# Score products over four column groups, a later first score episode, and pinned head work in a hybrid decoder layer

## The chip, the cores and the metric

The kernel runs on one NeuronCore of a Trainium2 chip. The metric is the device time of one execution in microseconds (us), lower is better. Engines are named as in the profile: PE is TensorE (matmuls, and PEld its weight loads), DVE is VectorE, ACT is ScalarE, POOL is GpSimd, SP is SyncE, which here only issues transfers.

## The reference, cut to what matters

One decoder layer on 1024 tokens of width 1024, all in 32-bit floats:

```python
x = x + hybrid_mixer(rms_norm(x, norm_mix), ...)                 # this half holds the change
x = x + square(relu(rms_norm(x, norm_mlp) @ w_up)) @ w_down
return rms_norm(x, norm_final)

# in hybrid_mixer
proj = h @ w_in                       # split into xa, ga, q, f, v, g, m_a, m_b, 1024 wide each
y_a = rg_lru(conv(xa), ...) * gelu(ga)
qf, kf = silu(q), (1 - lb) * sigmoid(-f);  log_f = log(lb + (1 - lb) * sigmoid(f))
o = rms_norm(hgrn2_chunkwise(qf, kf, log_f, v), hg_norm)         # 8 heads of 128
y = sigmoid(m_a) * y_a + sigmoid(m_b) * (o * silu(g))
return y @ w_out

# hgrn2_chunkwise, for each chunk of a head
o_inter = (q * exp(cum)) @ state
scores  = sum_k q[t] * k[s] * exp(cum[t] - cum[s])   for s <= t
o       = o_inter + scores @ v
state   = exp(last) * state + (k * exp(last - cum)).T @ v
```

The kernel uses chunks of 128 tokens instead of 32.

## The kernel before, in words

The tokens are done in two halves of 512 (`c` = 0, 1). In each half, four pairs of heads (`p` = 0 to 3) are done one after the other: these are the eight **stages**. A stage projects, in this order, `xa`, `q`, `f` (with the gates of the recurrent unit inside), `g`, `mb`, `ga` and `ma`; `v` is projected before every second stage. A projection (`project`) is 48 matmuls of 128x128 weights on 128x512 inputs: weights and inputs are split into a high and a low part, and each product is three matmuls (`mm3`, lines 121 to 123). It is two weight tiles ("halves") of eight **column groups**, where a group is one `mm3`, so three matmuls. The weights come by DMA, are cast on ACT (line 82, `wH`) and their low part is taken on DVE (line 83, `wL`).

The chunked recurrence is the generator `hgrn`. `gates` runs it in pieces between column groups: `next(scores)` once at its start, and then `project(c, name, at, do)` calls `go_on` after the group with number `at`. Its pieces before the change:

- Start: products of queries, keys and decays on DVE (line 467, a helper), up to the last part of `qa`.
- After group 8 of `mb`, the **first score episode**: 2 x 32 small matmuls (line 475; keys of 32 columns against 48 query columns), each writing a strip of 32 of a bank's 128 rows, chosen by `32 * b`. Then the two levels of `dd` masks on DVE (lines 490 to 499), the next level's `qb`, `kb`, `kk` (the keys, also called `kw`), `qn` (its last part is `q3`, line 572), `ke`.
- After group 7 of `ga`, everything else: the **second score episode** (lines 577 to 585: `p64` with 16 products 64 columns wide on strips 0 and 1, then `p8` with 32 products 48 wide on all four strips, then `p32` with 16 products 32 wide on strips 0 and 2), the third level's `dd` masks, copies into the score tile `scT` (POOL for `dd`, ACT for `p32` and `p64`), two DVE products and an ACT copy into `kk` (lines 603 to 605), `qf`; then for each head in turn the key transposes `pk` (line 623, copied to `kT` by ACT), key-value products `pkv` (line 629), outputs `po` (lines 636 and 639) and state updates `sn`, `scar` (lines 643 and 645).

What sets the order: a planner at build time orders each engine's instructions by priority and by its own estimate of when inputs are ready. `high_priority(300)` puts a piece run by `go_on` ahead of what was written up to 300 places before it. `turn` (`tc.keep_in_program_order`) pins an instruction behind the one written just before it on its engine; instructions written later may still be moved ahead of it. Score products are pinned; `pk`, `pkv`, `po` and the projections are not. On the chip each engine works through its order and waits where an input is late. PSUM banks (2 KB a partition): four with the tag `pj` for projections, two `sc`, two `hg`, each handed on when its last reader is done. `kT`, `sn`, `kb` are tiles with one buffer each.

Of the kernel before, what the change touches and what calls it, by code (L numbers as in the profile page):

```python
# [14 lines left out]
ALU = mybir.AluOpType  # L15
# [3 lines left out]
P = 128  # L19
D = 1024  # L20
S = 1024
T = 512
# [20 lines left out]
def trunk(ctx: ExitStack, tc: tile.TileContext, x, wts, mlp, pv, gains, mask_f, mask_u, out):  # L43
# [142 lines left out]
    def small_inputs():  # L186
        nc.sync.dma_start(pvt, pv[:, 0:PV_N])
        nc.sync.dma_start(mf, mask_f)
        mu32 = mt("kT", "mu32", (P, 4, P)).rearrange("p a b -> p (a b)")[:, : 7 * 32]
# [155 lines left out]

    def project(c, name, at=None, do=None):

        pp = [bank("pj", f"pj_{name}_{s}") for s in range(2)]
        for half in range(2):
            wh, wl = next_w()  # L350
            for k in range(4):
                hh, hl = kt(hT[c], 4 * half + k)
                for s in range(2):
                    cols = slice(k * 256 + s * P, k * 256 + (s + 1) * P)
                    mm3(pp[s], wh[:, cols], wl[:, cols], hh, hl, half == 0 and k == 0, half == 1 and k == 3)
                    if at == 8 * half + 2 * k + s:
                        do()
        return pp
# [105 lines left out]
    def hgrn(c, p, q1, f, kk, v):  # L464
# [131 lines left out]

        for b in (0, 2):
            A.copy(scT[32 * b : 32 * b + 32, :, 32 * b + 32 : 32 * b + 64], p32[32 * b : 32 * b + 32, :, :])
        A.copy(scT[0:64, :, 64:128], p64[0:64, :, :])
        t16 = t64.rearrange("p (a e) -> p a e", e=2)  # L600
        before = t16[:, :, 0:1].unsqueeze(3).to_broadcast([P, 8, 2, 32])
        after = t16[:, :, 1:2].to_broadcast([P, 8, 32])
# [14 lines left out]
        nkv = 3 if c + 1 == NC else 4  # L617
        pos = []
        for s in range(2):
            u = 2 * p + s  # L620
            pk = bank("hg", f"pk{c}{u}")
            for n in range(nkv):
                PE.transpose(pk[:, n * P : (n + 1) * P], kk[:, s * T + n * P : s * T + (n + 1) * P], ident)
            kT = mt("kT", f"kT{c}{u}", (P, 4, P))
            A.copy(kT[:, :nkv, :], pk[:, : nkv * P].rearrange("p (n k) -> p n k", n=nkv))
            pkv = bank("hg", f"pkv{c}{u}")
            vn = lambda n: v[:, n, (u % 4) * P : (u % 4 + 1) * P]
            for n in range(nkv):
                PE.matmul(pkv[:, n * P : (n + 1) * P], kT[:, n, :], vn(n), start=True, stop=True)
            sn = mt("sn", f"sn{c}{u}", (P, 3, P))  # L630
            state = lambda n: scar[:, u, :] if n in (0, 4) else sn[:, n - 1, :]
            po = bank("hg", f"po{c}{u}")
            for n in range(4):
                only = c == 0 and n == 0
                on_ps = po[:, n * P : (n + 1) * P]
                PE.matmul(on_ps, scT[:, 4 * s + n, :], vn(n), start=True, stop=only)
                if not only:
                    at = s * T + n * P
                    PE.matmul(on_ps, qf[:, at : at + P], state(n), start=False, stop=True)  # L639
                if n < nkv:  # L640
                    kv = pkv[:, n * P : (n + 1) * P]
                    if only:
                        V.tensor_copy(state(1), kv)
                    else:
                        V.scalar_tensor_tensor(
                            state(n + 1), state(n), t128[:, 4 * s + n : 4 * s + n + 1], kv, op0=ALU.mult, op1=ALU.add
                        )
            for n in range(4):
# [10 lines left out]
    def gates(c, p, h, scores, dst):  # L659
# [505 lines left out]
```

## Time and profile before

| | |
|---|---|
| median of 3 runs | 1599.73 us (1597.9 to 1602.51) |
| profiled execution | 1600.96 us, of which its span 1599.2 |
| PE busy | 1564.1 us, 98% of the span, 9002 matmul records |
| DVE busy | 1200.7 us, 75% |
| ACT busy | 784.9 us, 49% |
| DMA | 245.97 MB, mean 154 GB/s |
| mean granted TensorE clock | 0.996 |

A busy share is of one engine over the whole span. A row of a timeline gives start, duration, engine, line, operation, output and inputs with shapes, how many such instructions in a row were merged, and in brackets the idle time of the engine before it and what ended it. A row of the waits gives who waited for whom, the total, how often, and the longest. A matmul of 32-bit floats that are not split has two records; a split one has one.

### The profile page before, as it was taken

What the parts mean: (1) busy time and instruction counts of PE and PEld (TensorE: products, weight loads), DVE (VectorE), ACT (ScalarE), POOL (GpSimd) and SP (SyncE); (2) the same over time, 40 slices, a digit from 0 to 9 for tenths busy, and PEclk for the clock granted to TensorE, in tenths of its full rate; (3) what the DMA queues carried; (4) which work ended last, traced back from release to release, by engine and by line L of the source; (5) the groups of instructions that cost most, each with busy time, mean ns of one, the idle gap of its engine ahead of it and who ended that gap; (6) DMA issues with size and microseconds to landing.
All of it is one profiled execution on the core that took longest, in us unless ns stands there. A gap on an engine that the chain in (4) does not pass through costs nothing.

```text
span 1599.2 us, 22797 instructions
## 1 busy us (share of the span) xinstructions
PE 1564.1 (98%) x9002; PEld 1284.6 (80%) x9002; DVE 1200.7 (75%) x1748; ACT 784.9 (49%) x1241; POOL 74.7 (5%) x105
## 2 busy tenths in 40 slices
PE   9999999999999999999999997999999999999998
PEld 7788888787788888788788876888888878888886
DVE  5876954958652867846869687988788888888875
ACT  5644544546432644445445566766777731221115
POOL 1010000010000010000000000000000000000002
PEclk9999999999999999999999998999999999999999
DMA  6222222222243222222222362666666666666652
GB/s 233 88 80 92 93 68 92 97 76 93 80 167 136 93 67 92 93 80 92 80 80 93 127 206 102 252 254 254 240 244 256 227 261 233 256 247 249 254 222 106
DMA packets 57995, 245.97 MB, mean 154 GB/s; under 512 B 6816, under 2 KB 6944, under 8 KB 47136
## 3 DMA queue, kind: packets, MB, share of 16 engines
q1 hardware_dynamic: 56304, 239.27, 41.0%
q10 hardware_dynamic: 1584, 5.25, 0.9%
q8 instruction: 70, 1.15, 0.3%
q14 instruction: 37, 0.30, 0.1%
HBM read 184.72 MB, written 59.77 MB: 153 GB/s over the span
## 4 chain that ended last, share of the span: by engine, by line
PE 84%; DVE 12%; ACT 1%; issue 1%; DMA 1%; POOL 0%; SPq 0%; DVEq 0%; ACTq 0%; POOLq 0%
PE dX L121 3%; PE dX L123 3%; PE dX L122 3%; PE uX L121 3%; PE uX L122 3%; PE uX L123 3%; DVE wL L83 2%; PE pj_xa L122 2%; PE pj_ma L123 2%; PE pj_xa L121 2%; PE pj_ma L121 2%; PE pj_ma L122 2%; PE pj_xa L123 2%; PE pj_f L121 2%; PE pj_f L123 2%; PE pj_f L122 2%
## 5 line engine op out<-in xcount | busy, mean ns | idle before, releaser
L83 DVE TENSOR_TENSOR wL<-raw,wH 128x1024 fp32r<-128x1024 f32 x158 | 193.5, 1225 | 134.2 <-ACT wH L82 133.8
L82 ACT CAST wH<-raw 128x1024 fp32r<-128x1024 f32 x160 | 167.8, 1049 | 177.9 <-issue 38.8
L1075 DVE TENSOR_TENSOR acc<-acc,dX 128x512 f32<-128x512 f32 x128 | 86.8, 685 | 29.3 <-PE dX L123 29.3
L82 ACT CAST wA<-q 128x512 fp32r<-128x512 f32 x32 | 19.8, 621 | 128.7 <-PE dX L123 81.4
L1075 DVE TENSOR_TENSOR acc<-acc,dY 128x512 f32<-128x512 f32 x64 | 43.4, 685 | 16.0 <-PE dY L123 13.9
L428 DVE RECIPROCAL rr<-rr 128x512 f32<-128x512 f32 x16 | 53.6, 3347 | 0.0
L932 ACT ACTIVATE b<-b 128x512 f32<-128x512 f32 x48 | 30.2, 630 | 37.2 <-DVE b L931 37.2
L1036 POOL TENSOR_TENSOR acc<-acc,gain 128x512 f32<-128x512 f32 x8 | 10.4, 1298 | 610.9 <-ACT junk L1033 610.6
L649 ACT ACTIVATE on<-po 128x128 f32<-128x128 f32 x64 | 16.8, 277 | 44.2 <-PE po L639 44.2
L394 DVE SCALAR_TENSOR_TENSOR xc<-xp,pvt,xc 128x512 f32<-128x512 f32 x48 | 33.1, 747 | 0.0
L539 POOL TENSOR_SCALAR seg<-seg 128x128 f32<-128x128 f32 (+1 forms) x16 | 16.7, 1045 | 340.2 <-DVE seg L467 340.2
L933 ACT ACTIVATE b<-b 128x512 f32<-128x512 f32 x48 | 30.1, 630 | 1.1
L123 PE MATMUL pj_mb<-hT0H,wL 128*128 128x512 f32 x64 | 25.0, 391 | 1.5 <-issue 1.5
L122 PE MATMUL pj_ga<-hT0H,wH 128*128 128x512 f32 x64 | 25.8, 402 | 0.4 <-issue 0.4
L123 PE MATMUL pj_ga<-hT1H,wL 128*128 128x512 f32 x64 | 26.1, 407 | 0.0
L121 PE MATMUL uX<-h2B11L,wA 128*128 128x512 f32 x64 | 25.5, 399 | 0.3 <-DVE rstd_h L147 0.3
L121 PE MATMUL pj_ga<-hT0L,wH 128*128 128x512 f32 x64 | 25.8, 403 | 0.0
L123 PE MATMUL pj_ga<-hT0H,wL 128*128 128x512 f32 x64 | 25.7, 402 | 0.0
L121 PE MATMUL pj_ga<-hT1L,wH 128*128 128x512 f32 x64 | 25.4, 397 | 0.0
L121 PE MATMUL po<-wL,y0H 128*128 128x512 f32 x64 | 25.3, 398 | 0.1
L121 PE MATMUL pj_mb<-hT0L,wH 128*128 128x512 f32 x64 | 25.4, 397 | 0.0
L121 PE MATMUL pj_mb<-hT1L,wH 128*128 128x512 f32 x64 | 25.4, 396 | 0.0
(1889 smaller groups left out, 5203.4 us busy)
## 6 DMA issues: line engine op xcount, KB each, us to landing
raw<-wts_in SPq DMA_DIRECT2D x160, 512.0 KB, 3.3
q<-mlp_in SPq DMA_DIRECT2D x64, 512.0 KB, 3.6
x<-x_in SPq DMA_DIRECT2D x8, 512.0 KB, 5.8
acc<-x ACTq DMA_DIRECT2D x8, 512.0 KB, 5.9
y_out<-acc SPq DMA_DIRECT2D x16, 256.0 KB, 2.1
xs<-x_in SPq DMA_DIRECT2D x8, 256.0 KB, 4.2
x<-xs SPq DMA_DIRECT2D x8, 256.0 KB, 2.0
x2s<-x_in SPq DMA_DIRECT2D x4, 512.0 KB, 5.4
```

The costliest lines, as they stand in the source:

```text
L82: keep(A.copy(h, src))
L83: keep(engine.tensor_tensor(out=lo, in0=src, in1=h.bitcast(F32), op=ALU.subtract))
L121: keep(PE.matmul(o, ah, bl, start=first, stop=False, **how))
L122: keep(PE.matmul(o, ah, bh, start=False, stop=False, **how))
L123: keep(PE.matmul(o, al, bh, start=False, stop=last, **how))
L394: V.scalar_tensor_tensor(xc[:, s, :], xp[:, j : j + T], pvt[:, PV_CW + 8 * j + u : PV_CW + 8 * j + u + 1], xc[:, s, :], op0=ALU.mult, op1= ...
L428: V.reciprocal(rec, rec)
L539: G.tensor_scalar(after[:, :, 2], t4[:, :, 3], 1.0, 0.0, op0=ALU.mult, op1=ALU.add)
L649: A.activation(on[:, 4 * s + n, :], po[:, n * P : (n + 1) * P], AF.Square, accum_out=ssq[:, 4 * s + n : 4 * s + n + 1])
L932: A.activation(b[:, at, :], b[:, at, :], AF.Relu, scale=-1.0 if at == 2 else 1.0)
L933: A.activation(b[:, at, :], b[:, at, :], AF.Square)
L1075: V.tensor_tensor(out=dst, in0=dst, in1=banks[bk, pr], op=op)
```

## The change

- `project` takes a tuple of group numbers. The first score episode runs after group 10 of `mb` instead of 8. The second one stays after group 7 of `ga`, and the generator has three more stops: the transposes of both heads after group 9, the key-value products of both after 11, the outputs of both after 13.
- The second episode is one loop over eight blocks; in each, two 32-wide, two 64-wide and four 48-wide products, and `p64` now uses strips 1 and 3. The copy of `p64` into `scT` becomes two copies of 32 rows.
- The DVE products and the ACT copy into `kk` and the copies of `p32` are written ahead of the third level's masks.
- `pk`, `pkv` and `po` matmuls are pinned in written order. `pkv` uses `sc` banks; `kT` of both heads is one tile in the place of `kb`; `sn` holds both heads' states, and six state updates come ahead of the outputs (the last of each head behind them).
- The small mask `mu32` lands in the tile `sn` instead of `kT`.

```diff
-    def project(c, name, at=None, do=None):
+    def project(c, name, at=(), do=None):
...
-                    if at == 8 * half + 2 * k + s:
+                    if 8 * half + 2 * k + s in at:
                         do()
...
         p64 = bank("sc", f"sc64_{nm}").rearrange("p (n t) -> p n t", n=8)
+        p32 = bank("hg", f"sc32_{nm}")[:, :256].rearrange("p (n t) -> p n t", n=8)
+        p8 = bank("sc", f"sc8_{nm}")[:, : 8 * 48].rearrange("p (n t) -> p n t", n=8)
         for n in range(8):
-            for j, keys in ((0, ke[:, 2 * n, :]), (1, kw[:, 4 * n + 1, :])):
-                small(p64[32 * j : 32 * j + 32, n, :], keys, q3[:, n, 1:3, :])
-        p8 = blocks(kb, rhs, str(cw))
-        p32 = bank("hg", f"sc32_{nm}")[:, :256].rearrange("p (n t) -> p n t", n=8)
-        for n in range(8):
-            for b in (0, 2):
-                small(p32[32 * b : 32 * b + 32, n, :], kw[:, 4 * n + b, :], qv[:, 4 * n + b + 1, :])
+            k = 4 * n
+            small(p32[0:32, n, :], kw[:, k, :], qv[:, k + 1, :])
+            small(p64[32:64, n, :], ke[:, 2 * n, :], q3[:, n, 1:3, :])
+            small(p32[64:96, n, :], kw[:, k + 2, :], qv[:, k + 3, :])
+            small(p64[96:128, n, :], kw[:, k + 1, :], q3[:, n, 1:3, :])
+            for b in range(4):
+                small(p8[32 * b : 32 * b + 32, n, :], kb[:, 32 * (k + b) : 32 * (k + b) + 32], rhs(k + b))
...
+        mul(kw[:, 1::4, :], kw[:, 1::4, :], after)
+        mul(kw[:, 0::4, :], ke[:, 0::2, :], after)
+        A.copy(kw[:, 2::4, :], ke[:, 1::2, :])
+        for b in (0, 2):
+            A.copy(scT[32 * b : 32 * b + 32, :, 32 * b + 32 : 32 * b + 64], p32[32 * b : 32 * b + 32, :, :])
         level(li, cw, p8)
...
-        A.copy(scT[0:64, :, 64:128], p64[0:64, :, :])
...
-        mul(kw[:, 0::4, :], ke[:, 0::2, :], after)
-        mul(kw[:, 1::4, :], kw[:, 1::4, :], after)
-        A.copy(kw[:, 2::4, :], ke[:, 1::2, :])
+        for j in range(2):
+            A.copy(scT[32 * j : 32 * j + 32, :, 64:128], p64[64 * j + 32 : 64 * j + 64, :, :])
...
-            kT = mt("kT", f"kT{c}{u}", (P, 4, P))
-            pkv = bank("hg", f"pkv{c}{u}")
-            sn = mt("sn", f"sn{c}{u}", (P, 3, P))
...
+        sn = mt("sn", f"sn{nm}", (P, 6, P))
+        kT = mt("kb", f"kT{nm}", (P, 8, P))
...
+        yield
+        for s, u in enumerate(us):
+            pk = bank("hg", f"pk{c}{u}")
+            for n in range(nkv):
+                turn(PE.transpose(pk[:, n * P : (n + 1) * P], kk[:, s * T + n * P : s * T + (n + 1) * P], ident))
+            A.copy(kT[:, 4 * s : 4 * s + nkv, :], pk[:, : nkv * P].rearrange("p (n k) -> p n k", n=nkv))
+        yield
+        for s, u in enumerate(us):
+            pkvs.append(bank("sc", f"pkv{c}{u}"))
+            for n in range(nkv):
+                small(pkvs[s][:, n * P : (n + 1) * P], kT[:, 4 * s + n, :], vn(u, n))
+        for s in range(2):
+            for n in range(3):
+                step(s, n)
+        yield
+        for s, u in enumerate(us):
+            po = bank("hg", f"po{c}{u}")
...
+                turn(PE.matmul(on_ps, scT[:, 4 * s + n, :], vn(u, n), start=True, stop=only))
...
+                    turn(PE.matmul(on_ps, qf[:, at : at + P], state(s, n), start=False, stop=True))
+            if nkv == 4:
+                step(s, 3)
...
-        pb = project(c, f"mb{c}{p}", 8, go_on)
+        pb = project(c, f"mb{c}{p}", (10,), go_on)
...
-        pa = project(c, f"ga{c}{p}", 7, go_on)
+        pa = project(c, f"ga{c}{p}", (7, 9, 11, 13), go_on)
```

More of the change, by code (lines that the diff above doesn't have):

```diff
@@ L188, in small_inputs @@
         nc.sync.dma_start(mf, mask_f)
[L189 removed]
+        mu32 = mt("sn", "mu32", (P, 6, P)).rearrange("p a b -> p (a b)")[:, : 7 * 32]
         mu32 = mu32.rearrange("p (i b t) -> p i b t", i=7, b=1)
@@ L595, in hgrn @@
             )
[L597 to L602, printed above, removed]
-        mul(kw[:, 0::4, :], ke[:, 0::2, :], after)
-        mul(kw[:, 1::4, :], kw[:, 1::4, :], after)
-        A.copy(kw[:, 2::4, :], ke[:, 1::2, :])
+        for j in range(2):
+            A.copy(scT[32 * j : 32 * j + 32, :, 64:128], p64[64 * j + 32 : 64 * j + 64, :, :])
         qf = mt("q1", f"qf{nm}", (P, 1792))[:, 0:1024]
@@ L617, in hgrn, with step @@
         nkv = 3 if c + 1 == NC else 4
-        pos = []
-        for s in range(2):
-            u = 2 * p + s
+        us = (2 * p, 2 * p + 1)
+        vn = lambda u, n: v[:, n, (u % 4) * P : (u % 4 + 1) * P]
+        sn = mt("sn", f"sn{nm}", (P, 6, P))
+        state = lambda s, n: scar[:, us[s], :] if n in (0, 4) else sn[:, 3 * s + n - 1, :]
+        kT = mt("kb", f"kT{nm}", (P, 8, P))
+        pkvs = []
+        def step(s, n):
+            kv = pkvs[s][:, n * P : (n + 1) * P]
+            at = 4 * s + n
+            if c == 0 and n == 0:
+                V.tensor_copy(state(s, 1), kv)
+            else:
+                V.scalar_tensor_tensor(
+                    state(s, n + 1), state(s, n), t128[:, at : at + 1], kv, op0=ALU.mult, op1=ALU.add
+                )
+        yield
+        for s, u in enumerate(us):
             pk = bank("hg", f"pk{c}{u}")
             for n in range(nkv):
-                PE.transpose(pk[:, n * P : (n + 1) * P], kk[:, s * T + n * P : s * T + (n + 1) * P], ident)
-            kT = mt("kT", f"kT{c}{u}", (P, 4, P))
-            A.copy(kT[:, :nkv, :], pk[:, : nkv * P].rearrange("p (n k) -> p n k", n=nkv))
-            pkv = bank("hg", f"pkv{c}{u}")
-            vn = lambda n: v[:, n, (u % 4) * P : (u % 4 + 1) * P]
-            for n in range(nkv):
-                PE.matmul(pkv[:, n * P : (n + 1) * P], kT[:, n, :], vn(n), start=True, stop=True)
-            sn = mt("sn", f"sn{c}{u}", (P, 3, P))
-            state = lambda n: scar[:, u, :] if n in (0, 4) else sn[:, n - 1, :]
+                turn(PE.transpose(pk[:, n * P : (n + 1) * P], kk[:, s * T + n * P : s * T + (n + 1) * P], ident))
[3 more added lines that the diff above has]
+            pkvs.append(bank("sc", f"pkv{c}{u}"))
+            for n in range(nkv):
+                small(pkvs[s][:, n * P : (n + 1) * P], kT[:, 4 * s + n, :], vn(u, n))
[4 more added lines that the diff above has]
+        for s, u in enumerate(us):
             po = bank("hg", f"po{c}{u}")
```

13 lines of the change are left out of this document (3 added, 10 removed).

## The prediction

> **What bounds the kernel now.** I read the page first, then the waits of TensorE (PE), then the timelines of PE, VectorE (DVE) and ScalarE (ACT) in one of the eight stages (one per half of the sequence and pair of heads).
>
> ```profile
> span 1599.2 us, 22797 instructions
> PE 1564.1 (98%) x9002; PEld 1284.6 (80%) x9002; DVE 1200.7 (75%) x1748; ACT 784.9 (49%) x1241; POOL 74.7 (5%) x105
> PE sc L475 <- DVE qa L467: 6.5, 7, 0.9
> PE pk L623 <- DVE dd L499: 3.1, 7, 0.5
> ```
>
> PE is busy for 98% of the span, so PE time taken out shortens the kernel as long as no other engine's work becomes late. The two waits are at the first score episode and at the key transposes. A matmul's listed duration runs past the start of the next, so listed idle understates a wait; I take starts. PE in the third stage (start, duration):
>
> ```profile
> 302.05 0.39 PE L123 MATMUL pj_mb<-hT0H,wL 128*128 128x512 f32 x1
> ...
> 302.73 0.39 PE L123 MATMUL pj_mb<-hT0H,wL 128*128 128x512 f32 x1
> 304.07 0.88 PE L475 MATMUL sc<-qa,kb 128*32 128x48 f32 x63 [0.95 <-DVE qa L467]
> 304.75 0.21 PE L475 MATMUL sc<-q,kk 128*32 128x48 f32 x1
> 305.57 0.51 PE L121 MATMUL pj_mb<-hT0L,wH 128*128 128x512 f32 x1
> ...
> 315.69 0.39 PE L123 MATMUL pj_ga<-hT0H,wL 128*128 128x512 f32 x1
> 316.00 0.24 PE L475 MATMUL sc<-qn,ke 128*32 128x64 f32 x1
> ...
> 316.82 0.24 PE L475 MATMUL sc<-qb,kb 128*32 128x48 f32 x2
> 316.87 0.22 PE L475 MATMUL sc<-qn,ke 128*32 128x64 f32 x1
> ...
> 317.58 0.69 PE L475 MATMUL sc<-qn,kk 128*32 128x32 f32 x32
> 318.20 0.50 PE L121 MATMUL pj_ga<-hT0L,wH 128*128 128x512 f32 x1
> 318.53 0.39 PE L122 MATMUL pj_ga<-hT0H,wH 128*128 128x512 f32 x1
> ...
> 319.23 0.40 PE L122 MATMUL pj_ga<-hT0H,wH 128*128 128x512 f32 x1
> 320.07 0.63 PE L623 MATMUL pk<-ident,kk 128*128 128x128 f32 x4 [0.45 <-DVE dd L499]
> 320.46 0.48 PE L123 MATMUL pj_ga<-hT0H,wL 128*128 128x512 f32 x1
> ...
> 321.24 0.40 PE L123 MATMUL pj_ga<-hT0H,wL 128*128 128x512 f32 x1
> 321.48 1.06 PE L629 MATMUL pkv<-v,kT 128*128 128x128 f32 x8
> ```
>
> A projection matmul starts every 0.227 us (three steps from 302.05 to 302.73); a column group is three of them, 0.68. Where no input is late, a score episode starts 0.31 after the last projection matmul (315.69 to 316.00). After small work the second projection matmul comes 0.33 after the first (318.20 to 318.53), not 0.227: each return costs 0.1.
>
> DVE and ACT in the same stage:
>
> ```profile
> 303.22 0.70 DVE L467 TENSOR_TENSOR qa<-qa,seg 128x512 f32<-128x512 f32 x1
> ...
> 313.49 0.69 DVE L467 TENSOR_TENSOR qn<-qn,seg 128x512 f32<-128x512 f32 x1
> ...
> 316.96 1.23 DVE L83 TENSOR_TENSOR wL<-raw,wH 128x1024 fp32r<-128x1024 f32 x1 [1.48 <-ACT wH L82]
> 318.11 0.42 DVE L467 TENSOR_TENSOR kk<-kk,seg 128x256 f32<-128x256 f32 x1
> 318.44 0.37 DVE L499 COPY_PREDICATED dd<-mu,sc 128x192 f32<-128x192 uint8 x1
> ...
> 319.51 0.42 DVE L467 TENSOR_TENSOR kk<-ke,seg 128x256 f32<-128x256 f32 x1
> ...
> 317.14 0.58 ACT L599 COPY scT<-sc 64x512 f32<-64x512 f32 x1 [0.21 <-PE sc L475]
> 317.85 0.41 ACT L608 COPY qf<-qn 128x256 f32<-128x256 f32 x1
> 318.16 0.40 ACT L609 COPY qf<-qn 128x256 f32<-128x256 f32 x1
> 318.47 0.73 ACT L598 COPY scT<-sc 32x256 f32<-32x256 f32 x2
> ```
>
> **The change, part by part.**
>
> (a) First episode two groups (six matmuls) later. Today it should start at 302.73 + 0.31 = 303.04, but waits for the product into qa, which ends at 303.92, and starts 0.15 later at 304.07: 1.03 lost. Six matmuls later it would arrive at 303.04 + 6 x 0.227 = 304.40, 0.33 after its inputs. Here are the first and the last of the eight:
>
> ```profile
> 92.50 0.39 PE L123 MATMUL pj_mb<-hT0H,wL 128*128 128x512 f32 x1
> 93.12 0.29 PE L475 MATMUL sc<-qa,kb 128*32 128x48 f32 x7 [0.23 <-ACT wH L82]
> ...
> 869.84 0.39 PE L123 MATMUL pj_mb<-hT1H,wL 128*128 128x512 f32 x1
> 871.15 0.25 PE L475 MATMUL sc<-qa,kb 128*32 128x48 f32 x5 [0.93 <-DVE qa L467]
> ```
>
> The first stage loses 0.62 - 0.31 = 0.31, the last 1.00; with the seven alike, 0.31 + 7 x 1.03 = 7.5 us. What is late next would be the second episode, since there are now 39 matmuls between the two, not 45. It needs q3, the last part of qn, ready on DVE at 313.49 + 0.69 + 0.15 = 314.33. It would arrive at 304.40 + 1.50 (episode, 304.07 to 305.57) + 0.10 (return) + 39 x 0.227 + 0.08 = 314.93: 0.6 in hand. The DVE work that waits for the first episode (kb rewritten, then the first dd) follows a whole weight split; the episode ends 0.33 later than today, so I cost that at nothing, DVE's backlog being its cover; without that cover it costs up to 0.33 a stage.
>
> (b) Second episode over four column groups. Its keys are 32 columns wide, and the strip of 32 output rows they write is their column group. Today 16 products 64 wide run on two strips (316.00 to 316.82: 0.102 each per strip, eight on each), 32 products 48 wide on four (first half of the first episode, 304.07 to 304.75: 0.085), 16 products 32 wide on two (317.58 to 318.20: 0.077). In all 2.20. Dealt to four strips, the busiest holds eight of 64 and eight of 48: 8 x (0.102 + 0.085) = 1.50. That strips run by themselves, with mixed widths and two PSUM banks, shows at 316.82: 48-wide products start before the last 64-wide ones (316.87), on the strips these leave free. Bounds: an even load over the strips, 8 x (0.102 + 0.085 + 0.077 + 0.085)/2 = 1.40; all one after the other, 16 x 0.102 + 32 x 0.085 + 16 x 0.077 = 5.6. I take 1.50, nearest to the overlap seen: 8 x 0.70 = 5.6 us. One row pair speaks for a floor per record instead: the 64-wide part starts 32 records in 0.82, 26 ns each; against it, the first episode starts 128 in 1.50 us, 12 ns each. The Trainium skill (TensorE: Matmul & The Clock Gate, "Wait — 56ns, not 53.3ns?") has such a floor: matmul starts never fall below some 25 ns, however small the matmul. By that page, as an estimate, 128 records take 3.2 us and the sum would end 13.6 us higher; by the first episode it stays as it is, so the trace does not agree with the floor where four strips are in use.
>
> (c) Key transposes. Without a wait they would start at 319.23 + 0.24 (the entry at 321.24 to 321.48) = 319.47; they start at 320.07, since DVE, after a weight split that ends at 318.19, puts dd and qf work between its two kk products, the second of which ends at 319.93. So 0.60 a stage is lost. After: DVE's two kk products are issued ahead of dd and qf. The split hangs on ACT's cast, and that on PE's half of ga, so it still ends 2.19 after the episode's start; the first kk product starts at 2.11 (318.11 less 316.00), the second 0.33 on, as dd does now, and ends 0.42 later at 2.86, seen at 3.01. PE, with an episode of 1.50 and now six matmuls in between, arrives at 1.50 + 0.33 + 4 x 0.227 + 0.24 = 2.98. Nearly even; 8 x 0.60 = 4.8 us. What goes behind the kk products, dd and qf, comes up to 0.7 later; what waits for it is under (e).
>
> (d) Pinning. Both heads' transposes, then both key-value products, then both outputs, each after its own two groups. The same matmuls, but in the first half of the sequence four runs of projections instead of six after the second episode, 2 x 0.1 x 4 stages = 0.8 us. In the second half there are four now: nothing.
>
> (e) New waits. Eight transposes take 2 x 0.39 (320.07 to 320.46), and with a return and six matmuls the key-value products arrive at 2.98 + 0.78 + 0.10 + 1.36 = 5.2. They need kT. The score copy of 64 rows becomes two of 32, each at most the 0.58 of the old; ACT then has kk, two small scT copies, two large and two qf copies, 0.31 (the step from one qf copy to the next) + 0.73 + 1.16 + 0.62 = 2.8, from 1.65 after the episode's start to 4.5, and a first kT copy of the same width as the old 0.58 ends at 5.1. Nearly even. Then:
>
> ```profile
> 322.90 0.73 DVE L645 SCALAR_TENSOR_TENSOR sn<-sn,seg,pkv 128x128 f32<-128x128 f32 x2
> 320.22 1.78 POOL L588 TENSOR_SCALAR scT<-dd 32x256 f32<-32x256 f32 x4 [15.82 <-DVE dd L499]
> ```
>
> Four key-value products take 1.06 (321.48), so the second head's end at 5.2 + 2.12 = 7.3; three state updates of 0.37 behind them end at 8.4. The first output arrives at 7.3 + 0.1 + 1.36 = 8.8, and only the second head's outputs need the last updates. POOL's copies of dd end at 6.0 today and at most 0.7 later, 2 us ahead. So the new waits are between nothing and one order turned round, 0.6 a stage, as today's at pk. I take the low end, since all of these come out in hand, and allow 0.1: 0.8 us. No DMA is issued or moved, one small mask load merely lands in another tile; SP's queue and POOL's order stay.
>
> Sum: 7.5 + 5.6 + 4.8 + 0.8 - 0.8 = 17.9 us. The profiled execution took 1600.96 us, with 1.8 around its span of 1599.2; that gives 1583.1. It lies 1.2 above the median of 1599.73, so for the median 1582.
>
> **Rivals.**
>
> DVE keeps its order. The planner puts dd and qf between the two kk products as today. They then end 3.9 after the episode's start, PE arrives at 2.98: with the 0.15 to be seen, a wait of 1.05 a stage. That takes 8.4 back: 1590. For it: that is today's order. Against: both are traced ahead of dd now, and become ready with it.
>
> The wait moves to the second episode. A second weight split (1.23) falls into DVE's chain ahead of q3: 1.23 - 0.6 = 0.6 a stage, 4.9 in all, 1587; two splits 1.9 a stage, 1597. For it: DVE idles nowhere from the recurrent gates to q3. Against: splits are timed by PE, which moves the same way.
>
> The other side: strips of unlike width or bank do not overlap, each product waits for the one before. Then the episode takes 5.6, 3.4 more than today instead of 0.7 less: 1582 + 8 x 4.1 = 1615. It decides from 2.20 + 12.3/8 = 3.7 us on. Against it stand 316.82 and 316.87.
>
> A floor per record. If the dealt order keeps the 26 ns a record of today's 64-wide part, it takes 128 x 0.026 = 3.3: 1582 + 8 x 1.8 = 1596. Against it: the first episode's 12 ns.
>
> The pins do not give the written order. Projections written behind a pinned product may still be moved ahead of it. If the pieces drift so that (a), (c) and (d) bring nothing, (b) is left: 1599.7 - 5.6 = 1594; with (e) at its bound of 0.6 a stage, 1599. For it: today the transposes stand after the fifth matmul, not at a group's end. Against: both pinned episodes stand exactly where they are written.
>
> **How the numbers follow.** Forecast 0.70, its own range 1577 to 1587 (the runs shown spread 1597.9 to 1602.5, and (e) may cost nothing or twice what I allow). DVE order 0.12. Second episode late 0.06. Serial strips 0.05. Floor 0.02. Pins 0.05. The range 1576 to 1592 holds the first two and a part of the third. 0.3% of this kernel is 4.8 us, about what a measurement tells from no change: faster 0.70 + 0.12 + 0.05 (a late second episode short of 1595) = 0.87; same 0.06, from the floor and most of the pins; slower 0.07, the serial strips and the rest.
>
> **What would show it.** In the timeline after: the first episode 0.31 after its last matmul, in all eight stages; the second in about 1.5 us, 32-, 64- and 48-wide products mixed; transposes after six matmuls with no idle before; eight transposes, then two groups, and so on; the wait of sc for qa gone from the list and pk's near nothing. The prediction is wrong if sc waits for qn, if pk or pkv wait for kk or kT by over 0.5 us a stage, or if the second episode takes over 2 us.

## The result, and the profile after

The median fell from 1600.07 us (four runs, the three given above among them, 1597.9 to 1602.51) to 1584.14 us (four runs, 1582.06 to 1584.83), a ratio of 0.9891 with a 95% interval of 0.9879 to 0.9904. The forecast was 1582, its range 1576 to 1592. The profiled execution of the changed kernel took 1582.06 us with a span of 1579.3, 19.9 less than the span before.

The page of the changed kernel, and from PE's waits the rows at the places in question; the waits of `sc` for `qa` and of `pk` for `dd` are not in the list any more:

```profile
span 1579.3 us, 22822 instructions
PE 1554.5 (98%) x9002; PEld 1281.2 (81%) x9002; DVE 1199.7 (76%) x1748; ACT 789.4 (50%) x1249; POOL 75.0 (5%) x105
PE sc L475 <- DVE qn L467: 1.5, 2, 1.0
```

The kernel does the same work in the same number of matmul records, and PE is listed as busy for 98% of the span in both: a matmul's listed duration hides part of a wait, so what went shows in the starts. So I add up each stage from the start of its first `mb` matmul to the start of its first `ma` matmul. The third stage, PE, before:

```profile
296.84 0.39 PE L121 MATMUL pj_mb<-hT0L,wH 128*128 128x512 f32 x1
...
330.45 0.39 PE L121 MATMUL pj_ma<-hT0L,wH 128*128 128x512 f32 x1
```

and after:

```profile
292.60 0.39 PE L121 MATMUL pj_mb<-hT0L,wH 128*128 128x512 f32 x1
...
299.85 0.39 PE L123 MATMUL pj_mb<-hT0H,wL 128*128 128x512 f32 x1
300.17 0.89 PE L475 MATMUL sc<-qa,kb 128*32 128x48 f32 x64
...
310.41 0.39 PE L123 MATMUL pj_ga<-hT0H,wL 128*128 128x512 f32 x1
310.73 0.22 PE L475 MATMUL sc<-qn,kk 128*32 128x32 f32 x1
...
311.80 0.22 PE L475 MATMUL sc<-qn,ke 128*32 128x64 f32 x1
...
312.00 0.22 PE L475 MATMUL sc<-qn,ke 128*32 128x64 f32 x1
...
312.44 0.50 PE L121 MATMUL pj_ga<-hT0L,wH 128*128 128x512 f32 x1
...
313.71 0.40 PE L123 MATMUL pj_ga<-hT0H,wL 128*128 128x512 f32 x1
313.94 1.04 PE L642 MATMUL pk<-ident,kk 128*128 128x128 f32 x8
...
315.97 0.39 PE L123 MATMUL pj_ga<-hT0H,wL 128*128 128x512 f32 x1
316.19 1.95 PE L475 MATMUL pkv<-v,kT 128*128 128x128 f32 x16
...
319.13 0.39 PE L123 MATMUL pj_ga<-hT0H,wL 128*128 128x512 f32 x1
319.36 0.60 PE L658 MATMUL po<-v,scT 128*128 128x128 f32 x4
...
323.85 0.39 PE L121 MATMUL pj_ma<-hT0L,wH 128*128 128x512 f32 x1
```

The stage took 33.61 us before (330.45 - 296.84) and takes 31.25 now. The first episode starts 0.32 after the last matmul before it (299.85 to 300.17), so nothing is late. The second takes 1.71 (310.73 to 312.44); its 64-wide products on one strip repeat every 0.197 (311.80 to 312.00). Transposes, key-value products and outputs each start 0.22 or 0.23 after the matmul before them, which is the step between two projection matmuls: no wait at any of the three.

DVE in the same stage:

```profile
311.70 1.23 DVE L83 TENSOR_TENSOR wL<-raw,wH 128x1024 fp32r<-128x1024 f32 x1 [0.35 <-ACT wH L82]
312.84 0.42 DVE L467 TENSOR_TENSOR kk<-ke,seg 128x256 f32<-128x256 f32 x1
313.18 0.42 DVE L467 TENSOR_TENSOR kk<-kk,seg 128x256 f32<-128x256 f32 x1
313.51 0.37 DVE L499 COPY_PREDICATED dd<-mu,sc 128x192 f32<-128x192 uint8 x1
313.77 0.69 DVE L467 TENSOR_TENSOR qf<-qn,seg 128x512 f32<-128x512 f32 x1
```

The two `kk` products start 2.11 and 2.45 after the episode's start (310.73) and stand ahead of `dd` and `qf`, as the change writes them.

Summed over the stages, before: 32.89, 33.59, 33.61, 35.36, 33.73, 33.81, 33.77, 33.81, together 270.57 us. After: 31.25, 31.25, 31.25, 33.08 and four times 31.08, together 251.15. That is 19.4 of the 19.9 us that the span lost; nothing outside the stages moved by much. The medians differ by 15.9. The profiled execution is the shortest of the four; the other three had spans of 1581.2 to 1583.1 and left no trace, so where their 2 to 4 us lie is open.

The fourth stage stands out, 1.8 longer than its neighbours. PE there, then DVE:

```profile
402.67 0.39 PE L123 MATMUL pj_ga<-hT0H,wL 128*128 128x512 f32 x1
403.58 0.22 PE L475 MATMUL sc<-qn,kk 128*32 128x32 f32 x2 [0.53 <-DVE qn L467]
404.79 0.22 PE L475 MATMUL sc<-qn,ke 128*32 128x64 f32 x1 [0.98 <-DVE qn L467]
```

```profile
394.84 1.29 DVE L149 SCALAR_TENSOR_TENSOR xn<-x,rstd_x,gain 128x1024 f32<-128x1024 f32 x1 [0.53 <-POOL rstd_x L148]
...
403.36 0.68 DVE L467 TENSOR_TENSOR ke<-kk,seg 128x512 f32<-128x512 f32 x1
403.96 0.68 DVE L467 TENSOR_TENSOR qn<-qn,seg 128x512 f32<-128x512 f32 x1
```

The first norm of the second half (line 149, 1.29 us, behind 0.53 of idle until POOL has taken the norm's power, line 148) fell into DVE's chain between the two episodes. `q3`, the last `qn`, ends at 404.64, about 1.8 later than PE wanted it, and the episode starts late and then stops.

### The profile page after: what moved, and what is told of

Its sections match the earlier page's. It is cut to its first block, busy times and chain, and to the rows that moved or that the text cites. A ratio compares the mean times of both kernels' runs of the same rounds, so it can differ in the third digit from the quotient of the medians.

```text
span 1579.3 us, 22822 instructions
## 1 busy us (share of the span) xinstructions
PE 1554.5 (98%) x9002; PEld 1281.2 (81%) x9002; DVE 1199.7 (76%) x1748; ACT 789.4 (50%) x1249; POOL 75.0 (5%) x105
## 4 chain that ended last, share of the span: by engine, by line
PE 91%; DVE 6%; DMA 2%; issue 1%; ACT 1%; POOL 0%; SPq 0%; DVEq 0%; POOLq 0%
PE dX L121 4%; PE dX L123 3%; PE dX L122 3%; PE uX L121 3%; PE uX L123 3%; PE uX L122 3%; PE pj_ga L121 2%; PE pj_ma L123 2%; PE pj_xa L121 2%; PE pj_ma L122 2%; PE pj_ma L121 2%; PE pj_xa L122 2%; PE pj_xa L123 2%; PE pj_f L121 2%; PE pj_f L123 2%; PE pj_f L122 2%
## 5 line engine op out<-in xcount | busy, mean ns | idle before, releaser
L122 PE MATMUL uX<-h2B11H,wA 128*128 128x512 f32 x64 | 25.5, 398 | 0.0
L123 PE MATMUL uX<-h2B11H,wA 128*128 128x512 f32 x64 | 25.4, 396 | 0.0
L121 PE MATMUL po<-wL,y1H 128*128 128x512 f32 x64 | 25.2, 394 | 0.0
L121 PE MATMUL pv<-wL,hT1H 128*128 128x512 f32 x64 | 25.1, 394 | 0.0
```

The lines of the kernel that those rows point to most:

```text
L121: keep(PE.matmul(o, ah, bl, start=first, stop=False, **how))
L122: keep(PE.matmul(o, ah, bh, start=False, stop=False, **how))
L123: keep(PE.matmul(o, al, bh, start=False, stop=last, **how))
```

## The experiments

Ratios are against the kernel before on the same chip; the rows come from several chips, so compare ratios and not medians. Stage sums come from starts as above, in the one traced execution of each kernel. "First half" is a plain stage there (the third, or the first where that is disturbed), "second half" the seventh.

| kernel | ratio (95%) | median us | first half | second half | eight stages |
|---|---|---|---|---|---|
| before | 1 | 1600.07 | 33.61 | 33.77 | 270.57 |
| after | 0.9891 (0.9879 to 0.9904) | 1584.14 | 31.25 | 31.08 | 251.15 |
| late_only | 0.9955 (0.9942 to 0.9969) | 1594.6 | 32.58 | 32.79 | 263.33 |
| dealt_only | 0.9960 (0.9947 to 0.9974) | 1595.43 | 32.76 | 32.88 | 264.50 |
| at8 | 0.9925 (0.9909 to 0.9941) | 1588.48 | 32.30 | 32.10 | 257.07 |
| two_strips | 0.9932 (0.9918 to 0.9947) | 1589.57 | 31.95 | 31.76 | 257.06 |
| masks_first | 0.9914 (0.9897 to 0.9930) | 1586.95 | 31.57 | 31.35 | 254.43 |
| no_pins | 0.9922 (0.9907 to 0.9936) | 1587.51 | 32.14 | 31.91 | 258.45 |
| at12 | 0.9917 (0.9897 to 0.9938) | 1587.54 | 31.62 | 31.45 | 256.36 |
| norm_pinned | 0.9902 (0.9885 to 0.9919) | 1585.68 | 31.25 | 31.03 | 251.09 |
| strips_even | 0.9890 (0.9875 to 0.9906) | 1584.51 | 31.49 | 30.96 | 251.50 |
| both | 0.9899 (0.9878 to 0.9920) | 1584.64 | 31.48 | 30.95 | 250.99 |
| qf_late | 0.9899 (0.9877 to 0.9920) | 1585.76 | 31.33 | 31.22 | 255.44 |
| padded | 0.9974 (0.9962 to 0.9986) | 1598.85 | 31.25 | 31.07 | 249.29 |

None of these is faster than the changed kernel by more than the intervals allow.

**at8: the first episode back after group 8.**

```diff
-        pb = project(c, f"mb{c}{p}", (10,), go_on)
+        pb = project(c, f"mb{c}{p}", (8,), go_on)
```

> The changed kernel, with the first score episode back after group 8. Theory (late input): the episode again waits for the qa product, 1.0 us in seven stages and 0.3 in the first, as the trace of before shows, so 7.5 us of the gain go: about 1591.5 instead of 1584.1, and the list of waits has sc for qa again. Rival (planner): the gain is of the changed order as a whole, DVE's order moves too and less than 2 us are lost.

The wait of `sc` for `qa` is back, 6.6 us in seven stages. The first stage lost 0.32 and the regular ones 1.0 to 1.05, as expected; the whole is 5.9 and not 7.5, because the fourth stage became 0.5 shorter: its norm (line 149) now comes on DVE at 405.14, behind the start of the second episode (404.92), and is no longer in the chain ahead of it.

**late_only: the kernel before, with the first episode after group 10 and nothing else.**

```diff
-        pb = project(c, f"mb{c}{p}", 8, go_on)
+        pb = project(c, f"mb{c}{p}", 10, go_on)
```

> Before, with nothing but the first episode two groups later. Theory: entry loss 0.31 + 7 x 1.0 = 7.5 us goes and nothing comes in its place: stages sum to 263 us, ratio about 0.9953, 1592.5. The fourth stage of before also has a stop of 1.5 us put down to issue right after the first episode, which may go or stay. Rival: DVE's backlog shifts with the first episode and the second one or the key transposes take 0.33 a stage or more back: 265.7 us or more, 1595.

7.24 us in the stages, and nothing moves behind the episode: the second episode and the wait at the transposes stand where they were. In the fourth stage `sc` waits 1.8 for `qn`, which takes the place of the stop that this stage had before. So term (a) is right, alone as well as with the rest.

**two_strips: the changed kernel with the old order and strips of the second episode.**

```diff
-            small(p32[0:32, n, :], kw[:, k, :], qv[:, k + 1, :])
-            small(p64[32:64, n, :], ke[:, 2 * n, :], q3[:, n, 1:3, :])
...
+            for j, keys in ((0, ke[:, 2 * n, :]), (1, kw[:, 4 * n + 1, :])):
+                small(p64[32 * j : 32 * j + 32, n, :], keys, q3[:, n, 1:3, :])
```

> The changed kernel, with the second episode's products in the order and on the strips of before (64 wide on strips 0 and 1, then 48 wide on four, then 32 wide on strips 0 and 2), all else as changed. Theory (load of the strips): the episode takes 2.20 us again instead of the 1.71 measured, 0.49 x 8 = 3.9 us, about 1588. By the prediction's own term it would be 0.70 x 8 = 5.6 us, 1589.7. Rival: part of it was hidden, because the kk products end at the same time behind the weight split, and the transposes now come late enough for nothing to wait: then the loss is the same 3.9, but a wait at the transposes in the changed kernel would have eaten it; if so, under 2 us are lost.

The episode takes 2.19 again, 0.49 more, and the transposes wait 0.2, since the planner's order of DVE for this kernel has `dd` and `qf` between the two `kk` products, as before the change:

```profile
313.58 0.42 DVE L467 TENSOR_TENSOR kk<-kk,seg 128x256 f32<-128x256 f32 x1
313.92 0.37 DVE L499 COPY_PREDICATED dd<-mu,sc 128x192 f32<-128x192 uint8 x1
314.18 0.68 DVE L467 TENSOR_TENSOR qf<-qn,seg 128x512 f32<-128x512 f32 x1
314.78 0.42 DVE L467 TENSOR_TENSOR kk<-ke,seg 128x256 f32<-128x256 f32 x1
```

0.70 a stage in all. That it is the prediction's total for (b) is chance: 0.49 are the strips and 0.2 an order of DVE.

**dealt_only: the kernel before, with the four-strip order of the episode and nothing else.** The edit is the reverse of two_strips, made in the kernel before (with the two copies of `p64`).

> Before, with nothing but the four-strip order of the second episode (first episode, DVE's order and the pieces as before). The prediction priced this part by itself at 8 x 0.70 = 5.6 us; the changed kernel's episode shortens by 0.49, so 3.9 us (about 1596, ratio 0.9975) if the parts add. Theory: they do not. The second kk product ends 3.9 us after the episode's start whatever the episode takes, since it stands behind a weight split, dd and qf on DVE; an episode that ends 0.49 sooner only makes PE wait 0.49 longer at the key transposes, 1.1 instead of 0.6. Then the stages sum to 270 to 271 us as before and the time is 1599 to 1601. Rival, the parts add: 266.7 us in the stages.

Neither held. A regular stage became 0.85 shorter (33.61 to 32.76): 0.49 in the episode and 0.35 behind it. The planner answered the shorter episode with another order: the transposes now come after nine matmuls instead of five, and on DVE the second `kk` product comes ahead of `qf`.

```profile
318.01 0.42 DVE L467 TENSOR_TENSOR kk<-kk,seg 128x256 f32<-128x256 f32 x1
```

```profile
318.96 0.39 PE L123 MATMUL pj_ga<-hT0H,wL 128*128 128x512 f32 x1
319.45 0.66 PE L626 MATMUL pk<-ident,kk 128*128 128x128 f32 x4
```

```profile
318.99 0.41 ACT L608 COPY kk<-ke 128x256 f32<-128x256 f32 x1
```

My theory took DVE's order of before as given, and that was its error. DVE's part is done at 318.43, and what `pk` waits for now is ACT's copy into `kk`, which stands behind the score copies and ends at 319.40. The wait is 0.25 instead of 0.6 (318.96 to 319.45 is 0.49, without a wait 0.24). The change writes this copy ahead of the score copies, too.

**masks_first: the `kk` products and the copy into `kk` written behind the masks again.**

```diff
-        mul(kw[:, 1::4, :], kw[:, 1::4, :], after)
-        mul(kw[:, 0::4, :], ke[:, 0::2, :], after)
-        A.copy(kw[:, 2::4, :], ke[:, 1::2, :])
...
         A.copy(scT[32 * j : 32 * j + 32, :, 64:128], p64[64 * j + 32 : 64 * j + 64, :, :])
+        mul(kw[:, 1::4, :], kw[:, 1::4, :], after)
...
```

> The changed kernel, with the two DVE products and the ACT copy into kk written behind the third level's masks and the copies of p64, as before. Theory (DVE order): the kk products end behind dd and qf, some 3.9 us after the second episode starts, while PE arrives at the transposes 3.2 after it (1.71 for the episode as measured, then six matmuls): a wait of about 0.8 us in each of eight stages, 6 us in all, about 1590. Rival (distance): six matmuls between the episode and the transposes are enough by themselves, and the place of the kk products changes nothing, under 1 us.

3.3 us, of which 1.0 is a stop in the second stage (last section); a regular stage lost 0.3. But this run did not test the theory, since the order of DVE that it is about did not come. The planner put only the first mask between the two `kk` products and kept `qf` behind both, and it moved the transposes to the place after the ninth matmul. In the third stage, DVE and ACT:

```profile
313.50 0.42 DVE L467 TENSOR_TENSOR kk<-kk,seg 128x256 f32<-128x256 f32 x1
```

```profile
314.48 0.41 ACT L608 COPY kk<-ke 128x256 f32<-128x256 f32 x1
```

The second product ends at 313.92, and the transposes start at 314.94: they wait for ACT's copy into `kk`, which stands behind the score copies and ends at 314.89. They start 0.39 later than their nine matmuls account for, in the changed kernel 0.14 later than their six. So most of the 0.3 is the place of ACT's copy, as in dealt_only, and what the order of the `kk` products is worth by itself no run shows.

**no_pins: `pk`, `pkv` and `po` not pinned.**

```diff
-                turn(PE.transpose(pk[:, n * P : (n + 1) * P], kk[:, s * T + n * P : s * T + (n + 1) * P], ident))
+                PE.transpose(pk[:, n * P : (n + 1) * P], kk[:, s * T + n * P : s * T + (n + 1) * P], ident)
```

and so for the other three calls.

> The changed kernel without pins on the transposes, key-value products and outputs (their three stops in the generator stay). Theory (place): without pins the planner puts the transposes after the fifth matmul again, 0.2 us early for the kk products, and splits the outputs by single projection matmuls, each return 0.1 us: 0.3 to 0.5 us a stage, 2 to 4 us in all, 1586 to 1588. Rival (the stops do it): the order is as with pins and nothing changes, under 1 us.

More than expected: 7.3 us, 0.8 to 0.9 a regular stage and 0.5 more in the second, where PE stops for its instructions (last section). PE in the third stage:

```profile
315.58 0.39 PE L123 MATMUL pj_ga<-hT0H,wL 128*128 128x512 f32 x1
316.31 1.06 PE L642 MATMUL pk<-ident,kk 128*128 128x128 f32 x8 [0.33 <-DVE kk L467]
...
317.94 1.60 PE L648 MATMUL pkv<-v,kT 128*128 128x128 f32 x12
319.51 0.49 PE L658 MATMUL po<-v,scT 128*128 128x128 f32 x2
```

The transposes are brought forward to the third matmul, where the second `kk` product is not done, and the outputs are mixed in between and straight behind the key-value products. DVE keeps the order of the changed kernel. The transposes start 0.61 later than their three matmuls account for, instead of 0.14 with six: 0.47 of the loss in a regular stage is a wait that the pinned matmuls cover. The rest lies in the mixed pieces behind and is not taken apart.

**at12: the first episode two groups later still.**

```diff
-        pb = project(c, f"mb{c}{p}", (10,), go_on)
+        pb = project(c, f"mb{c}{p}", (12,), go_on)
```

> The changed kernel, with the first episode after group 12 instead of 10. PE arrives at the second episode at the same time as with 10, but DVE's products that wait for the first episode start 1.36 us later. Theory (slack): in the changed kernel's third stage the second episode starts 0.37 us after its last input could have been used, and DVE's chain is some 0.8 us behind the first episode, so about 0.6 of the 1.36 reach q3 and 0.2 to 0.4 a stage are lost, 2 to 3 us in all, as a wait of sc for qn. Rival (DVE has room): nothing changes, within 1 us.

0.37 in every regular stage, at the upper end of what was expected, but not as a wait of `sc` for `qn`: with 33 matmuls between the episodes PE would be ahead of `q3`, and the planner puts one projection matmul into the second episode, which then takes 2.32 instead of 1.71, with 0.23 of it the step of that matmul. Two stages lost 1.6 us more, put down to "issue" (last section), and the fourth became 0.6 shorter.

**norm_pinned: the first norm of the second half pinned to its place in the written order.**

```diff
+        in_order[0] = True
         rows(0)
+        in_order[0] = False
```

> The changed kernel, with the first row block of the second half's norm pinned behind the work written before it. In the changed kernel's fourth stage that norm (1.29 us on DVE and 0.53 of idle for POOL) stands in DVE's chain between the two episodes, and the second episode starts late and stops once. Theory: with the norm out of the chain, the fourth stage loses its waits, 33.08 to 31.25 us from the start of mb to that of ma, 1.8 us of the whole; the norm's own chain then starts later, but there is an output projection of 22 us to cover it. Rival: the first use of the norm waits instead, and the 1.8 us come back there.

The fourth stage fell from 33.08 to 31.26 as expected, so the norm was its cause. The gain did not stay: PE waits for the output projection's sum instead, whose DVE work was held up by a late load,

```profile
PE po L121 <- DVE xs L740: 1.5, 1, 1.5
```

```profile
459.97 1.33 DVE L740 TENSOR_TENSOR xs<-po,xs 128x512 f32<-128x512 f32 x2 [6.35 <-DMA xs<-x_in]
```

and the second stage became 1.8 longer by a stop that the changed kernel did not have:

```profile
198.33 0.29 PE L477 MATMUL sc<-qb,kb 128*32 128x48 f32 x4
200.17 0.23 PE L477 MATMUL sc<-qb,kb 128*32 128x48 f32 x1 [1.55 <-issue]
200.33 0.50 PE L121 MATMUL pj_ga<-hT0L,wH 128*128 128x512 f32 x1
```

**padded: norm_pinned with 35 narrow matmuls more in the warm-up at the start.** They add work; nothing else differs.

```diff
         pace(7)
+        for _ in range(35):
+            keep(PE.matmul(warm[:, 0:8], ones[:, 0, :], ones[:, 0, 0:8], start=True, stop=True))
```

> norm_pinned with 35 narrow matmuls (two records and two weight loads each, 140 instructions of PE) more in the warm-up at the start, so that each later instruction stands 140 places further on. Theory: PE's program comes in blocks of 256 instructions; a score episode is 256 instructions in 1.4 to 1.6 us, and where a block begins with the episode, the next one is not there when the episode has used it up. In norm_pinned the block ends at place 254 of the second stage's second episode (1.55 us lost there); here it ends at place 114. Then the second stage is 31.25 like the others, and the sum 249.4 against 251.09; the nearest to such a place is now the sixth stage's second episode (place 236), where up to 1.5 us may be lost in its place. The warm-up itself takes up to 3 us more, so the time tells less than the stages: 1582 to 1587. Rival: the loss at about 200 us comes from something that happens there at that time (a transfer, a clock step), and the second stage still loses 1.5 us.

All eight stages are now alike: 31.25 four times, then 31.07 or 31.08, 249.29 together against 249.4 expected. The second stage's stop is gone and none came up elsewhere. The padding also moves everything about 14 us later in time, so by itself this run does not tell the place in the program from the time of the stop; the other kernels do (last section). The price of the padding was mis-sized: the 70 records took 14.94 us at the start, 0.21 each though 8 columns wide, so the time is no measure here.

```profile
4.18 14.94 PE L286 MATMUL warm<-ones 128*128 128x8 f32 x70
```

**strips_even: the 64-wide products on strips 1 and 3 in even blocks and 0 and 2 in odd ones, the 32-wide on the others.**

```diff
-            small(p32[0:32, n, :], kw[:, k, :], qv[:, k + 1, :])
-            small(p64[32:64, n, :], ke[:, 2 * n, :], q3[:, n, 1:3, :])
...
+            k, o, e = 4 * n, 32 * (n % 2), 32 - 32 * (n % 2)
+            small(p32[o : o + 32, n, :], kw[:, k, :], qv[:, k + 1, :])
+            small(p64[e : e + 32, n, :], ke[:, 2 * n, :], q3[:, n, 1:3, :])
...
```

> The changed kernel, with the 64-wide products on strips 1 and 3 for even blocks and 0 and 2 for odd ones, the 32-wide ones on the others, so that all four strips hold the same load; the four copies into scT become eight of half the width. Theory (load of the busiest strip): a block now takes (0.112 + 0.085 + 0.077 + 0.085)/2 = 0.18 instead of 0.197 us, so the episode takes about 1.57 instead of 1.71, 1.1 us over eight stages, if ACT's added copies make nothing late. Rival (a floor per record): 128 records at 13.4 ns stay 1.71. Second rival: ACT's added copies delay kT and 1 to 3 us are lost.

The episode fell from 1.71 to 1.52, near the 1.57 that the load of the busiest strip gives, and a minimum of 13.4 ns a record is refuted: 128 records in 1.52 us are 12 ns each. The first episode has 128 in 1.50, so a minimum of 12 ns is not excluded. But the score copies are now eight half-sized ones on ACT and end later, `kT` with them: in the first half the key-value products start 0.27 later behind the transposes and run 0.11 longer, which takes the 0.19 back and more (31.49 against 31.25). The second half, with a smaller transposed tile, keeps 0.12.

**both: norm_pinned and strips_even together.**

> The pinned norm and the even strips together. If the two act in different stages and on different causes, the gains add: 1.8 + 1.1 = 2.9 us under the changed kernel. Rival: the added ACT copies cost what the strips bring, and only the 1.8 of the norm is left.

250.99 us in the stages: the fourth at 31.49 like its neighbours, the second at 32.76 with the stop, and the waits for `xs` as in norm_pinned. The parts do as they did singly and bring nothing together.

**qf_late: strips_even, with the two `qf` copies written behind the copies of `kT`.**

```diff
-        A.copy(qw[:, :, 0, :], qv4[:, :, 0, :])
-        A.copy(qw[:, :, 1, :], q3[:, :, 0, :])
...
             A.copy(kT[:, 4 * s : 4 * s + nkv, :], pk[:, : nkv * P].rearrange("p (n k) -> p n k", n=nkv))
+        A.copy(qw[:, :, 0, :], qv4[:, :, 0, :])
+        A.copy(qw[:, :, 1, :], q3[:, :, 0, :])
```

> The changed kernel with two more edits: the load evened over the four strips (as in strips_even) and ScalarE's two qf copies moved behind the copies of kT. Theory: in strips_even ScalarE's backlog ahead of kT took the shorter episode's 0.19 us back; two qf copies are 0.62 us of that backlog, so the waits of +0.27 and +0.11 in the first-half stages go: 31.05 us a stage in the first half (1.8 more in the fourth), 30.9 in the second, sum about 249.5 against 251.15, time about 1582.5. Rival: what holds kT are the eight score copies and not qf, then the stages stay as in strips_even, 251.5; or the outputs now wait for qf, and the stages are longer than 251.5.

It did not test what it was built for. ACT's copies are not pinned, and the planner put them ahead of the score copies:

```profile
314.49 0.41 ACT L593 COPY kk<-ke 128x256 f32<-128x256 f32 x1 [0.65 <-PE sc L475]
314.81 0.40 ACT L646 COPY qf<-qn 128x256 f32<-128x256 f32 x1
315.11 0.40 ACT L647 COPY qf<-qn 128x256 f32<-128x256 f32 x1
315.42 1.06 ACT L597 COPY scT<-sc 32x128 f32<-32x128 f32 x4
```

Key-value products no longer wait, but the transposes take 1.01 instead of 0.79, and the second stage lost 3.5 with a stop of 2.0. Whether ACT's backlog is what strips_even pays for stays argued, not shown.

## Why the prediction was right, point by point

The effects that the prediction named for (a) to (c) are the ones that the traces show; but the sizes of (b) and (d) were well off, and that the total came out near is in part luck.

- **(a) First episode, 7.5 us:** 7.24 by itself, and about 1.0 a regular stage when taken out. Cover by DVE's backlog, costed at nothing, held: the second episode starts 0.32 after its last matmul in seven stages of eight.
- **(b) Second episode, 5.6 us:** mis-sized; 8 x 0.49 = 3.9. That mixed widths on four strips overlap was right. The price of a 64-wide product was not: I read 0.102 a strip from 316.00 to 316.82, but 316.82 is where the next bank's products started on free strips, while 64-wide records still started at 316.87. The block of the changed kernel repeats every 0.197, so 0.112 + 0.085; in the kernel before, too, the 64-wide products of one strip start 0.11 apart (at 316.25, 316.36 and 316.48). And eight blocks of 0.197 are 1.58; the last block needs 0.13 more before a projection can start, which I left out. 1.71 and not 1.50. The rival of a floor per record (3.3) is refuted by 1.71 and by strips_even's 1.52; so is the rival of strips one after the other (5.6). The Trainium skill (TensorE: Matmul & The Clock Gate, "Wait — 56ns, not 53.3ns?") has a least step of some 25 ns between matmul starts, by which, as an estimate, 128 records would take 3.2 us; across four strips the runs here do not agree with it.
- **(c) Transposes, 4.8 us:** right in size: from the end of the second episode they start 0.14 later than the matmuls in between account for, instead of 0.74, in every stage. What brings it is only in part separated. In the kernel before they waited for DVE, as predicted. But the change also writes ACT's copy into `kk` ahead of the score copies, which (c) does not price, and where that copy is late (dealt_only, masks_first) it is what the transposes wait for, some 0.25 of the 0.6 a stage. The rival that DVE keeps its order did not come true in the changed kernel; its price was not measured.
- **(d) Pins, 0.8 us:** too small. What is left of a stage's gain after (a) to (c) is put here. In the first half that is 0.25 a stage, as worked out for four stretches of projections instead of six. In the second half the prediction counted four before and after and forecast nothing, and some 0.64 a stage came: key-value products and outputs there take 4.74 instead of 5.29. That this is because they change less often from one kind of piece to the next is likely but not shown; banks and tiles changed with the order. Together 3.6. no_pins shows how much hangs on the pins: 7 us, since unpinned pieces are brought forward. "The pins do not give the written order" was the rival; they do.
- **(e) New waits, -0.8 us:** none at `pk`, `pkv` or `po`; the allowance was not needed. One wait of another kind came: 1.8 in the fourth stage, where a job fell into DVE's chain ahead of `q3`. That is the rival "the wait moves to the second episode" in one stage of eight, with the norm in the place of the weight split that I had named, and a wait of `sc` for `qn` is also one of the prediction's own signs of being wrong.

In the stages of the two traces: 7.3 + 3.9 + 4.8 + 3.6 = 19.6; a stop for instructions of 1.75 in the fourth stage of before went (last section), 1.83 came there for the norm: 19.5, and 19.4 was measured. Neither of these two was foreseen, and that they cancel is luck. (b) was 1.7 too large, (d) 2.8 too small and (e) 0.8 too careful, and that these partly made up for each other is luck, too: 17.9 forecast against 19.4 in the traced execution and 15.9 between the medians.

## What to carry to other kernels

Where an input is late by a known time on one engine and the waiting engine has other work, moving the piece behind that work brought the length of the wait each time ((a), 7.24 of 7.5 us forecast); pin the piece as well, since a planner that is free to reorder brought the same pieces forward into waits (no_pins, 7 us). Where one input of a piece comes earlier, look at its other inputs: behind DVE's `kk` products stood ACT's copy. Price small matmuls on column strips by the busiest strip and one block's tail, from rows that end when the last record of that width has started. When a part is taken out or done alone, look at the new order before crediting the part: in dealt_only, masks_first and qf_late the planner's answer was as large as the edit.

## What the runs showed of the hardware that I had not expected

PE stops for its own instructions. In all kernels here, every long stop of PE put down to "issue" near a score episode lies behind the same kind of place: counting PE's matmul records, weight loads and semaphore instructions in order of start from 0, behind instruction 2752, 4288 or 5312, each 256 n + 192. The instruction queue of the page fits blocks of 256. The changed kernel, then padded, which has 140 instructions more:

```profile
q8 instruction: 70, 1.15, 0.3%
```

```profile
q8 instruction: 71, 1.16, 0.3%
```

70 packets are 16 KB each; PE's some 18,100 instructions make 70.7 blocks of 256, and padded's some 18,250 make 71.3. (The changed kernel has one more packet behind its span, so this count alone is weak; the places of the stops are the stronger sign.) A score episode is 128 records and 128 weight loads, so one block, used up in 1.5 to 2.2 us. Where a block begins with the episode, the next one is needed at its end. In the changed kernel that block's packet came at 192.22, 4.5 us before the second stage's second episode began; in norm_pinned, with the block ending at the same instruction, at 197.55, 0.7 after the episode's start. The packet's row in windows of the two kernels, 192 to 193.2 and 197.5 to 198.7:

```profile
q8 instruction: 1, 0.02, 4.6%
```

```profile
q8 instruction: 1, 0.02, 5.6%
```

In the first the episode ran through (1.71); in the second PE stopped for 1.55 and went on at 200.17. at12 has two such stops, with packets at 198.75 and 314.64 and PE going on at 201.05 and 316.95, 2.3 after each packet's start (2.6 in norm_pinned). Shifting the boundary by 140 instructions (padded) took the stop away. All fourteen traces agree: with packet n (from 0) for the block behind instruction 256 n + 448, PE goes on 2.2 to 2.8 us after the start of the block's packet at all thirteen such stops, and where a packet started 2.9 us or more ahead of its block there is none near an episode. The stops come between 198 and 203, at 317 and at 401 to 402 us, so it is not one moment of the run. The Trainium skill (Runtime: NRT & Kernel Launch, "Instruction fetch mechanics") gives the same block, 16 KiB or 256 instructions, fetched while the one before runs, and calls the cost of a crossing "mostly hidden": the size agrees with these traces, and hidden it is at most crossings, but not where the packet comes late for a block that is needed at the end of an episode. In the changed kernel it came 6.1 us ahead of its block. What decides when a block's packet is sent, and so why it came that early there, the runs do not show. With 0.4 to 2.0 us of listed idle a time it is of the size of the experiments' smaller effects. The second stage of eight kernels carries 1.1 us or more of it: two_strips, masks_first, no_pins, at12, norm_pinned, both, qf_late and dealt_only; that of before (0.4) and of late_only (0.6) has a smaller one. The fourth stage of before has one, too (1.75), and that the traced execution of the changed kernel has none is part of the gain in the stages without being the work of any of its parts.
